# Root mean squares divided out after the projections instead of before the transposes

## The chip, the cores and the metric

The kernel runs on one core of one Trainium2 chip. The metric is the device time of one execution in microseconds (us). Five engines matter here: PE (TensorE, with its weight loads shown as PEld), DVE (VectorE), ACT (ScalarE), POOL (GpSimd) and SP, which issues most of the transfers.

## What is computed

Two stacks of blocks follow each other on 256 rows (tokens) of width 1024. Each block normalises its rows, multiplies them by one or more weight matrices, mixes them (state-space, recurrent, retention, sparse or cross attention, experts, or a gated feed-forward block) and adds the result to the rows. All arithmetic is float32. The norm ahead of a projection is

```
def rms_norm_2(x, g, eps=EPS):
    y = x * lax.rsqrt(jnp.mean(x * x, axis=-1, keepdims=True) + eps)
    return y * g

def swiglu(x, w_gate, w_up, w_down):
    return (jax.nn.silu(x @ w_gate) * (x @ w_up)) @ w_down
```

The factor `rsqrt(...)` is one number per row, and `g` one number per column of `x`. So the product `(x * r * g) @ w` equals `r * ((x * g) @ w)`: the factor per row may be applied before the product or to its result.

## The kernel before, in words

The rows lie in SBUF as `h`: 128 partitions, two token halves (`tt` = 0, 1), 1024 columns. A projection needs them transposed, with columns on the partitions; `normed` (L400) makes that. For each token half ACT squares and sums two halves of a row (L363), DVE adds them (L368), POOL raises the sum to the power -1/2 (L369), and DVE multiplies the identity by it, which gives the diagonal matrix `diag` (L409). PE then multiplies eight 128x128 blocks of `h` by `diag` (L411): each block comes out transposed and divided in one product. A float32 product takes two passes of PE, so the sixteen blocks of a norm are 32 records in the trace. Four PSUM banks of the small pool (`sm`, four banks) hold the eight transposed chunks. `put` (L382) then takes each chunk out of PSUM, multiplied by the column's gain, as two float32r parts: ACT writes the rounded value `xT_hi` (L385), DVE what is left, `xT_lo` (L386).

Weights stream from memory in units of 512 KB (L284). ACT rounds each unit to `whi` (L277, three buffers), and DVE takes the remainder `wlo` (L279, two buffers). `mm3` (L287) multiplies with three float32r products per chunk (L290, L291, L292). `fm_proj` (L294) gives results with columns on partitions, two units of 128 columns per PSUM bank; `tm_proj` (L309) gives them with rows on partitions, 512 columns per bank. Both hand a finished bank to an evacuation function. The large PSUM pool (`mm`) has four banks.

There are seventeen calls of `normed`. Eleven stand ahead of a projection touched here: `odd_mixer` (L793), two of `xattn` (L902), four of `ffn` (L1213), two of `xattn2` (L1263), `even_mixer2` (L1283) and `odd_mixer2` (L1626). The other six are the first mixer's, the two of the expert blocks and three for the memory rows. In the second stack each of the blocks but the last calls a `filler` after its norm: a piece of the keys' or values' projection of the memory, which does not depend on `h`.

The order of instructions on each engine is fixed when the program is built. A planner simulates the engines and, whenever an engine is free, gives it the ready instruction that comes first in the program (`later` shifts that position). On the chip each engine runs its own list strictly in that order and waits at semaphores, so an instruction that is ready later than the planner thought holds up all that stands behind it on its engine.

Of the kernel before, what the change touches and what calls it, by code (L numbers as in the profile page):

```python
# [9 lines left out]
F32 = mybir.dt.float32  # L10
# [11 lines left out]
P = 128  # L22
T = 256
# [181 lines left out]
class Kern:  # L205
# [159 lines left out]
    def row_rstd(self, ss, scale=1.0):  # L365

        r = self.small.tile([P, 1], F32, tag="rstd", name="rstd")
        self.nc.vector.tensor_scalar(r, ss[:, 0:1], ss[:, 1:2], EPS / scale ** 2, op0=ALU.add, op1=ALU.add)  # L368
        self.nc.gpsimd.tensor_tensor(r, r, self.mhalf[:, :1], op=ALU.pow)  # L369
        return r  # L370

    def rms_rows(self, src, tt):

        ss = self.small.tile([P, 2], F32, tag="ss", name="ss")
        for nb in range(2):
            self.square_sum(ss[:, nb:nb + 1], src[:, tt, nb * 512:nb * 512 + 512])
        return self.row_rstd(ss)
# [22 lines left out]
    def normed(self, src, gain, pool, name, dst=None):  # L400


        nc = self.nc
        dst = dst or self.parts(pool, 8, name)
        ps = [self.bank([P, 2, T]) for _ in range(4)]
        for tt in range(NT):
            r = self.rms_rows(src, tt)
            dg = self.small.tile([P, P], F32, tag="diag", name="diag")
            nc.vector.tensor_scalar(dg, self.ident, r, None, op0=ALU.mult)  # L409
            for c in range(8):  # L410
                nc.tensor.matmul(ps[c // 2][:, c % 2, tt * P:tt * P + P], src[:, tt, c * P:c * P + P], dg,  # L411
                                 start=True, stop=True)
        for c in range(8):
            self.put(dst, c, ps[c // 2][:, c % 2], self.col(gain, c))
        return dst

# [350 lines left out]
    def odd_mixer(self, norm_memory, filler):  # L767
        nc = self.nc
        with ExitStack() as es:
# [22 lines left out]
            with self.pool("odd_p") as pp:  # L792
                xT = self.normed(self.h, "norm_mix1", pp, "xT")  # L793

                def ev_f(j, ps, m):
                    nc.scalar.activation(kd[:, j:j + m], ps, AF.Sigmoid, scale=-1.0)
                    nc.scalar.activation(gc[:, j:j + m], ps, AF.Sigmoid)
                    for c in range(j, j + m):
                        nc.vector.tensor_scalar(kd[:, c], kd[:, c], om[:, c:c + 1], None, op0=ALU.mult)
                        nc.vector.tensor_scalar(gc[:, c], gc[:, c], om[:, c:c + 1], lb[:, c:c + 1],  # L800
                                                op0=ALU.mult, op1=ALU.add)
                self.fm_proj(xT, "od_f", range(8), ev_f)
                self.fm_proj(xT, "od_q", range(8),
                             lambda j, ps, m: nc.scalar.activation(qd[:, j:j + m], ps, AF.Silu))
# [21 lines left out]
                with self.later(200):  # L826
# [3 lines left out]
                self.tm_proj(xT, "od_i", lambda nb, tt, ps: nc.scalar.copy(  # L830
                    v[:, tt, nb * 512:nb * 512 + 512], ps))
                self.tm_proj(xT, "od_g", lambda nb, tt, ps: nc.scalar.activation(
                    gs[:, tt, nb * 512:nb * 512 + 512], ps, AF.Silu))
# [62 lines left out]
    def xattn(self, l, kT, v):  # L896
        nc = self.nc
        with self.pool("xa") as po:
            oT = self.parts(po, 8, "oT")
            with self.pool("xaq") as pq, self.pool("att_t", 2) as pt:  # L900
                qT = pq.tile([P, 8, T], F32, name="qT")
                xT = self.normed(self.h, f"norm_xattn{l}", pq, "xT")  # L902

                def head(j, ps, m):
                    nc.scalar.copy(qT[:, j:j + m], ps)
                    self.attend(j // 2, qT[:, j:j + 2], kT[:, j:j + 2], v, 1.0 / 16, oT, pt)
                self.fm_proj(xT, f"xa_q{l}", range(8), head)
            self.tm_proj(oT, f"xa_o{l}", self.add_to_h)
# [299 lines left out]
    def ffn(self, l, f, filler):  # L1208
        nc = self.nc
        with self.pool("ffn") as po:  # L1210
            aT = self.parts(po, 22, "aT")
            with self.pool("ffn_x") as px, self.pool("ffn_t", 2) as pt:
                xT = self.normed(self.h, f"ng{l}{6 if f else 0}", px, "xT")  # L1213
                filler()
                G, U = self.d(f"ff_g{l}{f}"), self.d(f"ff_u{l}{f}")
                for j in range(22):
# [6 lines left out]
                    a = pt.tile([P, T], F32, tag="a", name="a")  # L1223
                    nc.scalar.activation(a, ps[:, 0], AF.Silu)
                    nc.vector.tensor_tensor(a, ps[:, 1], a, op=ALU.mult)
# [31 lines left out]
    def xattn2(self, l, kT, v, filler):  # L1257
        nc = self.nc
        with self.pool("xa") as po:
            oT = self.parts(po, 4, "oT")  # L1260
            with self.pool("xaq") as pq, self.pool("att_t", 2) as pt:
                qT = pq.tile([P, 4, T], F32, name="qT")
                xT = self.normed(self.h, f"ng{l}4", pq, "xT")  # L1263
                filler()

                def heads(j, ps, m):
                    nc.scalar.copy(qT[:, j:j + m], ps)
# [5 lines left out]
    def even_mixer2(self, filler):  # L1273
        nc = self.nc
        with ExitStack() as es:
# [6 lines left out]
            with self.pool("ev2_x") as px, self.pool("ev2_raw", 2) as pr:  # L1282
                xT = self.normed(self.h, "ng02", px, "xT")  # L1283
                filler()
                with self.pool("rw_p") as pp:
                    rw = pp.tile([P, 14, T], F32, name="rw")

                    def shift(j, ps, m):
                        raw = pr.tile([P, 2, T + 1], F32, tag="raw", name="raw")
                        nc.vector.memset(raw[:, :, 0:1], 0.0)  # L1290
                        nc.scalar.copy(raw[:, :, 1:], ps)
# [6 lines left out]
                self.tm_proj(xT, "rt_qkv", lambda nb, tt, ps: nc.scalar.copy(  # L1298
                    qkv[:, tt, nb * 512:nb * 512 + 512], ps))
                self.fm_proj(xT, "rt_g", range(4), lambda j, ps, m: nc.scalar.activation(rg[:, j:j + m], ps, AF.Silu))  # L1300
# [319 lines left out]
    def odd_mixer2(self, filler):  # L1620
        nc = self.nc
        with self.pool("od2") as po:
            yT = self.parts(po, 8, "yT")
            pin = po.tile([P, NT, 456], F32, name="pin")
            with self.pool("od2_x") as px, self.pool("od2_t", 2) as pt:
                xT = self.normed(self.h, "ng12", px, "xT")  # L1626
# [5 lines left out]
                def ev_u(j, ps, m):  # L1632
                    t = pt.tile([P, T], F32, tag="t", name="t")
                    nc.scalar.copy(t, ps[:, 0])
                    nc.vector.tensor_tensor(u[:, j, 2:], ps[:, 1], t, op=ALU.mult)
# [7 lines left out]
                def ev_b(j, ps, m):  # L1643
                    for s in range(2):
# [4 lines left out]
                self.tm_proj(xT, "dsa_in", lambda nb, tt, ps: nc.scalar.copy(pin[:, tt], ps), n=456)  # L1649
# [162 lines left out]
```

## Time and profile before

| what | before |
|---|---|
| median of 3 runs (lowest to highest) | 3619.4 us (3611.51 to 3620.52) |
| the profiled execution | 3621.81 us |
| its span, first to last instruction | 3620.0 us |
| PE busy | 3510.9 us, 97% |
| DVE busy | 2404.2 us, 66% |
| ACT busy | 1781.6 us, 49% |
| mean granted clock of PE | 0.986 |

The shares are averages over very different stages. PE's records overlap, because its products are pipelined: one record of 256 columns lasts about 0.28 us, while the next starts some 0.12 us after it. A product of PE that waits for a semaphore shows as idle time of PE before it. The granted clock is 1.00 at the full 2.4 GHz and 0.50 at 1.2 GHz.

### The profile page before, as it was taken

What the parts mean: (1) busy time and instruction counts of PE and PEld (TensorE: products, weight loads), DVE (VectorE), ACT (ScalarE), POOL (GpSimd) and SP (SyncE); (2) the same over time, 40 slices, a digit from 0 to 9 for tenths busy, and PEclk for the clock granted to TensorE, in tenths of its full rate; (3) what the DMA queues carried; (4) which work ended last, traced back from release to release, by engine and by line L of the source; (5) the groups of instructions that cost most, each with busy time, mean ns of one, the idle gap of its engine ahead of it and who ended that gap; (6) DMA issues with size and microseconds to landing.
All of it is one profiled execution on the core that took longest, in us unless ns stands there. A gap on an engine that the chain in (4) does not pass through costs nothing. (4 is left out here: it accounts for less than half of the span.)

```text
span 3620.0 us, 60017 instructions
## 1 busy us (share of the span) xinstructions
PE 3510.9 (97%) x23584; PEld 3182.2 (88%) x23584; DVE 2404.2 (66%) x4051; ACT 1781.6 (49%) x2695; POOL 77.8 (2%) x93
## 2 busy tenths in 40 slices
PE   8999999999999999999999999999999999999899
PEld 8888999998888888899998888898898898987797
DVE  7655988977555754888986655555665555557554
ACT  6644444444444844445444444544523544444543
POOL 0000000000000000000000000000001000000000
PEclk9999999999999999999999999999998999999999
DMA  5444456668666544456668766566402455553355
GB/s 162 152 140 149 143 180 194 203 199 296 192 187 190 166 134 134 158 176 189 202 209 265 219 189 188 166 185 187 146 26 80 144 192 175 186 195 105 107 186 163
DMA packets 176835, 620.60 MB, mean 171 GB/s; under 512 B 19868, under 2 KB 20636, under 8 KB 175784
## 3 DMA queue, kind: packets, MB, share of 16 engines
q1 hardware_dynamic: 164000, 584.00, 52.0%
q10 hardware_dynamic: 12552, 32.78, 2.5%
q8 instruction: 184, 3.01, 0.3%
q14 instruction: 99, 0.81, 0.1%
HBM read 594.68 MB, written 22.02 MB: 170 GB/s over the span
## 5 line engine op out<-in xcount | busy, mean ns | idle before, releaser
L279 DVE TENSOR_TENSOR wlo<-wraw,whi 128x1024 fp32r<-128x1024 f32 x1058 | 1293.8, 1223 | 857.3 <-PE ps L292 316.3
L277 ACT CAST whi<-wraw 128x1024 fp32r<-128x1024 f32 x1058 | 1110.0, 1050 | 981.5 <-PE ps L291 705.4
L292 PE MATMUL ps<-xT_hi,wlo 128*128 128x256 f32 x4432 | 1253.5, 283 | 14.9 <-DVE wlo L279 14.0
L290 PE MATMUL ps<-xT_hi,whi 128*128 128x256 f32 x4432 | 1261.4, 285 | 0.9 <-ACT whi L277 0.8
L291 PE MATMUL ps<-xT_lo,whi 128*128 128x256 f32 x4432 | 1254.6, 283 | 0.5
L292 PEld LDWEIGHTS ps<-xT_hi,wlo 128*128 128x128 f32 x4432 | 836.1, 189 | 23.3 <-DVE wlo L279 21.3
L290 PEld LDWEIGHTS ps<-xT_hi,whi 128*128 128x128 f32 x4432 | 837.2, 189 | 5.5 <-ACT xT_hi L385 2.2
L291 PEld LDWEIGHTS ps<-xT_lo,whi 128*128 128x128 f32 x4432 | 836.9, 189 | 3.6 <-DVE xT_lo L386 2.3
L290 PE MATMUL ps<-whi,gh 128*128 128x512 f32 x1024 | 405.8, 396 | 3.6 <-ACT gh L1071 3.6
L291 PE MATMUL ps<-wlo,gh 128*128 128x512 f32 x1024 | 405.4, 396 | 0.0
L292 PE MATMUL ps<-whi,gl 128*128 128x512 f32 x1024 | 405.4, 396 | 0.0
L1071 ACT CAST gh<-H 128x256 fp32r<-128x256 f32 x256 | 104.1, 407 | 366.6 <-PE ps L291 364.7
L290 PEld LDWEIGHTS ps<-whi,gh 128*128 128x128 f32 x1024 | 193.3, 189 | 50.1 <-ACT gh L1071 4.0
L292 PEld LDWEIGHTS ps<-whi,gl 128*128 128x128 f32 x1024 | 193.3, 189 | 46.4 <-DVE gl L1073 0.5
L291 PEld LDWEIGHTS ps<-wlo,gh 128*128 128x128 f32 x1024 | 193.4, 189 | 46.0
L292 PE MATMUL ps<-whi,aT_lo 128*128 128x512 f32 x352 | 138.9, 395 | 0.0
L290 PE MATMUL ps<-whi,aT_hi 128*128 128x512 f32 x352 | 138.9, 394 | 0.0
L291 PE MATMUL ps<-wlo,aT_hi 128*128 128x512 f32 x352 | 138.8, 394 | 0.0
L1026 DVE TENSOR_TENSOR hot<-keys,i1T 128x1024 f16<-128x1024 f16 x64 | 130.4, 2037 | 0.0
L369 POOL TENSOR_TENSOR rstd<-rstd,mhalf 128x1 f32<-128x1 f32 x52 | 51.5, 990 | 2949.3 <-DVE rstd L368 2945.8
L1073 DVE TENSOR_TENSOR gl<-H,gh 128x256 fp32r<-128x256 f32 x256 | 107.4, 420 | 0.9 <-ACT gh L1071 0.9
L411 PE MATMUL ps<-diag,h 128*128 128x128 f32 x448 | 66.8, 317 | 42.3 <-DVE diag L409 39.8
(625 smaller groups left out, 4137.4 us busy)
## 6 DMA issues: line engine op xcount, KB each, us to landing
wraw<-in_peer_u_dram SPq DMA_DIRECT2D x256, 512.0 KB, 3.8
wraw<-in_peer_v_dram SPq DMA_DIRECT2D x256, 512.0 KB, 4.3
wraw<-in_ff_g_dram SPq DMA_DIRECT2D x88, 512.0 KB, 3.5
wraw<-in_ff_u_dram SPq DMA_DIRECT2D x88, 512.0 KB, 3.5
wraw<-in_ff_d_dram SPq DMA_DIRECT2D x88, 512.0 KB, 3.7
G<-late ACTq DMA_DIRECT2D x64, 320.0 KB, 4.5
g<-G SPq DMA_DIRECT2D x64, 320.0 KB, 4.9
wraw<-in_peer_q_dram SPq DMA_DIRECT2D x32, 512.0 KB, 3.6
```

What stands on the lines that cost most here:

```text
L277: nc.scalar.copy(hi, src)
L279: nc.vector.tensor_sub(lo, src, hi.bitcast(F32))
L290: mm(out, a[0], b[0], start=start, stop=False)
L291: mm(out, a[0], b[1], start=False, stop=False)
L292: mm(out, a[1], b[0], start=False, stop=stop)
L369: self.nc.gpsimd.tensor_tensor(r, r, self.mhalf[:, :1], op=ALU.pow)
L411: nc.tensor.matmul(ps[c // 2][:, c % 2, tt * P:tt * P + P], src[:, tt, c * P:c * P + P], dg, start=True, stop=True)
L1026: nc.vector.tensor_tensor(o1, keys[:, :, 0][:, None, :].to_broadcast([P, TOP, P]), i1T[:, t0:t0 + TOP, None].to_broadcast([P, TOP, P]), op ...
L1071: nc.scalar.copy(gh, src)
L1073: nc.vector.tensor_sub(gl, src, gh.bitcast(F32))
```

## The change

A new function `turned` takes the place of `normed` in eleven calls. It transposes the rows undivided, with PE's transposes against the identity, and puts them into the two parts with the gain as before. After that it makes `r`, the factor per row, with the same squares, sum and power. One product per token half with `r` spread over the stationary operand writes `r` along the free axis on all partitions, and ACT copies it to SBUF as `row`. It returns the transposed parts, `r` and a function `divide`.

Where a projection gives columns on partitions, `divide` multiplies the finished bank by `row` on DVE as it leaves PSUM. In `xattn`, `xattn2` and `even_mixer2` (`shift`) it takes the place of a copy on ACT; in `odd_mixer` (`ev_f`, `ev_q`), `even_mixer2` (`gate`), `ffn` and `odd_mixer2` (`ev_b`) it is an operation more; in `ev_u` it covers both halves of the bank, where before ACT copied one half. Where a projection gives rows on partitions, ACT's copy or Silu out of PSUM takes `r` as its scale per partition.

```
...
-    def row_rstd(self, ss, scale=1.0):
-        r = self.small.tile([P, 1], F32, tag="rstd", name="rstd")
+    def row_rstd(self, ss, scale=1.0, r=None):
+        r = self.small.tile([P, 1], F32, tag="rstd", name="rstd") if r is None else r
...
-    def rms_rows(self, src, tt):
+    def rms_rows(self, src, tt, r=None):
...
-        return self.row_rstd(ss)
+        return self.row_rstd(ss, 1.0, r)
...
+    def turned(self, src, gain, pool, name):
+        nc = self.nc
+        dst = self.parts(pool, 8, name)
+        for c in range(0, 8, 2):
+            ps = self.bank([P, 2, T])
+            for tt in range(NT):
+                for s in range(2):
+                    nc.tensor.transpose(ps[:, s, tt * P:tt * P + P], src[:, tt, (c + s) * P:(c + s) * P + P], self.ident)
+            for s in range(2):
+                self.put(dst, c + s, ps[:, s], self.col(gain, c + s))
+        r = pool.tile([P, NT], F32, name="r")
+        row = pool.tile([P, 1, T], F32, name="row")
+        ps = self.bank([P, T])
+        for tt in range(NT):
+            self.rms_rows(src, tt, r[:, tt:tt + 1])
+            nc.tensor.matmul(ps[:, tt * P:tt * P + P], r[:, tt:tt + 1].to_broadcast([P, P]), self.ident, start=True, stop=True)
+        nc.scalar.copy(row[:, 0], ps)
+        return dst, lambda tt: r[:, tt:tt + 1], lambda out, ps: nc.vector.tensor_tensor(
+            out, ps, row.to_broadcast([P, ps.shape[1], T]), op=ALU.mult)
...
-                xT = self.normed(self.h, "norm_mix1", pp, "xT")
+                xT, r, divide = self.turned(self.h, "norm_mix1", pp, "xT")
...
-                    nc.scalar.activation(kd[:, j:j + m], ps, AF.Sigmoid, scale=-1.0)
-                    nc.scalar.activation(gc[:, j:j + m], ps, AF.Sigmoid)
+                    f = gc[:, j:j + m]
+                    divide(f, ps)
+                    nc.scalar.activation(kd[:, j:j + m], f, AF.Sigmoid, scale=-1.0)
+                    nc.scalar.activation(f, f, AF.Sigmoid)
...
-                self.fm_proj(xT, "od_q", range(8),
-                             lambda j, ps, m: nc.scalar.activation(qd[:, j:j + m], ps, AF.Silu))
+                def ev_q(j, ps, m):
+                    divide(qd[:, j:j + m], ps)
+                    nc.scalar.activation(qd[:, j:j + m], qd[:, j:j + m], AF.Silu)
+                self.fm_proj(xT, "od_q", range(8), ev_q)
...
-                self.tm_proj(xT, "od_i", lambda nb, tt, ps: nc.scalar.copy(
-                    v[:, tt, nb * 512:nb * 512 + 512], ps))
+                self.tm_proj(xT, "od_i", lambda nb, tt, ps: nc.scalar.activation(
+                    v[:, tt, nb * 512:nb * 512 + 512], ps, AF.Copy, scale=r(tt)))
...
-                    gs[:, tt, nb * 512:nb * 512 + 512], ps, AF.Silu))
+                    gs[:, tt, nb * 512:nb * 512 + 512], ps, AF.Silu, scale=r(tt)))
...
-                xT = self.normed(self.h, f"norm_xattn{l}", pq, "xT")
+                xT, _, divide = self.turned(self.h, f"norm_xattn{l}", pq, "xT")
...
-                    nc.scalar.copy(qT[:, j:j + m], ps)
+                    divide(qT[:, j:j + m], ps)
...
-                xT = self.normed(self.h, f"ng{l}{6 if f else 0}", px, "xT")
+                xT, _, divide = self.turned(self.h, f"ng{l}{6 if f else 0}", px, "xT")
...
-                    a = pt.tile([P, T], F32, tag="a", name="a")
-                    nc.scalar.activation(a, ps[:, 0], AF.Silu)
-                    nc.vector.tensor_tensor(a, ps[:, 1], a, op=ALU.mult)
+                    gu = pt.tile([P, 2, T], F32, tag="gu", name="gu")
+                    divide(gu, ps)
+                    a = gu[:, 0]
+                    nc.scalar.activation(a, a, AF.Silu)
+                    nc.vector.tensor_tensor(a, gu[:, 1], a, op=ALU.mult)
...
-                xT = self.normed(self.h, f"ng{l}4", pq, "xT")
+                xT, _, divide = self.turned(self.h, f"ng{l}4", pq, "xT")
...
-                    nc.scalar.copy(qT[:, j:j + m], ps)
+                    divide(qT[:, j:j + m], ps)
...
-                xT = self.normed(self.h, "ng02", px, "xT")
+                xT, r, divide = self.turned(self.h, "ng02", px, "xT")
...
-                        nc.scalar.copy(raw[:, :, 1:], ps)
+                        divide(raw[:, :, 1:], ps)
...
-                self.tm_proj(xT, "rt_qkv", lambda nb, tt, ps: nc.scalar.copy(
-                    qkv[:, tt, nb * 512:nb * 512 + 512], ps))
-                self.fm_proj(xT, "rt_g", range(4), lambda j, ps, m: nc.scalar.activation(rg[:, j:j + m], ps, AF.Silu))
+                self.tm_proj(xT, "rt_qkv", lambda nb, tt, ps: nc.scalar.activation(
+                    qkv[:, tt, nb * 512:nb * 512 + 512], ps, AF.Copy, scale=r(tt)))
+                def gate(j, ps, m):
+                    divide(rg[:, j:j + m], ps)
+                    nc.scalar.activation(rg[:, j:j + m], rg[:, j:j + m], AF.Silu)
+                self.fm_proj(xT, "rt_g", range(4), gate)
...
-                xT = self.normed(self.h, "ng12", px, "xT")
+                xT, r, divide = self.turned(self.h, "ng12", px, "xT")
...
-                    t = pt.tile([P, T], F32, tag="t", name="t")
-                    nc.scalar.copy(t, ps[:, 0])
-                    nc.vector.tensor_tensor(u[:, j, 2:], ps[:, 1], t, op=ALU.mult)
+                    t = pt.tile([P, 2, T], F32, tag="t", name="t")
+                    divide(t, ps)
+                    nc.vector.tensor_tensor(u[:, j, 2:], t[:, 0], t[:, 1], op=ALU.mult)
...
+                    divide(cy[:, j - 4:j - 2], cy[:, j - 4:j - 2])
...
-                self.tm_proj(xT, "dsa_in", lambda nb, tt, ps: nc.scalar.copy(pin[:, tt], ps), n=456)
+                self.tm_proj(xT, "dsa_in", lambda nb, tt, ps: nc.scalar.activation(
+                    pin[:, tt], ps, AF.Copy, scale=r(tt)), n=456)
...
```

## Rows read from the trace of the kernel before

**Rows 1.** The profile's page, engines: busy us, share of the span, instructions

```profile
PE 3510.9 (97%) x23584; PEld 3182.2 (88%) x23584; DVE 2404.2 (66%) x4051; ACT 1781.6 (49%) x2695; POOL 77.8 (2%) x93
```

**Rows 2.** Waits of PE, whole span: who, for whom, us in total, times, longest

```profile
PE ps L411 <- DVE diag L409: 39.8, 13, 9.4
PE ps L292 <- DVE wlo L279: 16.9, 29, 2.9
...
PE ps L411 <- DVE rstd L368: 2.5, 3, 1.1
```

**Rows 3.** Timeline of PE at norms: start, us, engine, line, shapes, count [idle before, releaser]

```profile
288.08 3.76 PE L411 MATMUL ps<-diag,h 128*128 128x128 f32 x31 [1.93 <-DVE diag L409]
...
357.95 3.71 PE L411 MATMUL ps<-diag,h 128*128 128x128 f32 x30 [1.93 <-DVE diag L409]
...
1193.11 2.89 PE L411 MATMUL ps<-diag,h 128*128 128x128 f32 x16 [3.57 <-DVE diag L409]
1196.34 2.49 PE L411 MATMUL ps<-diag,h 128*128 128x128 f32 x15 [0.34 <-DVE diag L409]
...
2304.83 6.41 PE L411 MATMUL ps<-diag,h 128*128 128x128 f32 x32 [7.75 <-DVE diag L409]
...
2843.16 4.04 PE L411 MATMUL ps<-diag,h 128*128 128x128 f32 x32 [0.97 <-DVE diag L409]
...
3417.22 6.59 PE L411 MATMUL ps<-diag,h 128*128 128x128 f32 x32 [8.49 <-DVE diag L409]
```

**Rows 4.** Timeline of PE, one set of sixteen transposes

```profile
145.11 1.91 PE L396 MATMUL ps<-ident,ybuf 128*128 128x128 f32 x16
```

**Rows 5.** Timeline of DVE, last writes of the rows ahead of four norms

```profile
287.14 0.68 DVE L345 TENSOR_TENSOR h<-ps,h 128x512 f32<-128x512 f32 x1
...
1189.15 1.28 DVE L345 TENSOR_TENSOR h<-ps,h 128x512 f32<-128x512 f32 x2
...
2302.23 1.41 DVE L1184 SCALAR_TENSOR_TENSOR h<-h,rstd,g 128x512 f32<-128x512 f32 x2 [0.73 <-POOL rstd L369]
...
3414.61 1.42 DVE L1204 SCALAR_TENSOR_TENSOR h<-y,rstd,h 128x512 f32<-128x512 f32 x2 [0.44 <-POOL rstd L369]
```

**Rows 6.** Timeline of POOL, two of four powers at one norm

```profile
2509.41 1.40 POOL L369 TENSOR_TENSOR rstd<-rstd,mhalf 128x1 f32<-128x1 f32 x1 [1.72 <-DVE rstd L368]
2512.53 0.55 POOL L369 TENSOR_TENSOR rstd<-rstd,mhalf 128x1 f32<-128x1 f32 x1 [1.72 <-DMA masks<-in_c_masks_dram]
```

**Rows 7.** Groups by line, 2500 to 2560: busy us, mean ns, idle before

```profile
L1291 ACT COPY raw<-ps 128x512 f32<-128x512 f32 x6 | 3.5, 578 | 0.0
...
L386 DVE SCALAR_TENSOR_TENSOR xT_lo<-ps,cols,xT_hi 128x256 fp32r<-128x256 f32 x8 | 3.4, 479 | 1.3 <-ACT xT_hi L385 1.3
...
L1199 DVE TENSOR_TENSOR y<-ps,g 128x512 f32<-128x512 f32 x2 | 1.4, 689 | 2.5 <-ACT junk L363 2.5
```

**Rows 8.** Timeline of DVE in a feed-forward block, one pair of weight units

```profile
2350.25 1.22 DVE L279 TENSOR_TENSOR wlo<-wraw,whi 128x1024 fp32r<-128x1024 f32 x1 [1.71 <-PE ps L292]
2351.47 0.42 DVE L1225 TENSOR_TENSOR a<-ps,a 128x256 f32<-128x256 f32 x1
2352.37 0.43 DVE L1227 TENSOR_TENSOR aT_lo<-a,aT_hi 128x256 fp32r<-128x256 f32 x1 [0.47 <-ACT aT_hi L1226]
2353.07 1.23 DVE L279 TENSOR_TENSOR wlo<-wraw,whi 128x1024 fp32r<-128x1024 f32 x1 [0.28 <-PE ps L292]
```

**Rows 9.** Stretches: busy (instructions) PE, PEld, DVE, ACT, POOL; PEclk, DMA, GB/s

```profile
145.00:147.00 2.00, 2.00 (x19) 1.90 (x18) 0.48 (x1) 1.14 (x3) 0.00 (x0) 1.00 0.36 51
1194.20:1197.50 3.30, 2.96 (x14) 2.67 (x14) 0.71 (x3) 2.27 (x7) 1.10 (x2) 0.50 0.25 101
2300.10:2310.20 10.10, 5.37 (x25) 5.37 (x26) 4.44 (x13) 6.25 (x17) 2.75 (x5) 0.50 0.36 123
2320.00:2420.00 100.00, 100.00 (x836) 100.00 (x835) 56.73 (x70) 49.43 (x70) 0.00 (x0) 1.00 0.61 182
3412.80:3423.00 10.20, 5.79 (x27) 5.79 (x28) 4.08 (x10) 2.59 (x8) 2.50 (x3) 0.50 0.17 51
```

## The prediction

> **What bounds the kernel now.** I read the page's engine line first: PE is busy for 3510.9 of 3620.0 us [rows 1], so the end is set by how much PE has to do and by 109 us in which it stands. The list of PE's waits comes next. Its longest entries are the diagonal matrix of the norms and the remainder of the weights, `wlo` [rows 2]. The norms' entries are 39.8 and 2.5 us, 42.3 in all. Of these 9.4 us is the first norm of the program and 3.9 us belongs to the two expert blocks (1.93 in the row at 357.95, which stands for two), and neither is changed [rows 2, 3]. That leaves 29.0 us of waiting ahead of the eleven changed norms.
>
> The third view is PE's timeline at those norms [rows 3]. Each shows an idle piece, then 32 passes in one block. At the full clock the block lasts 4.04 us, a pass every (4.04 - 0.28) / 31 = 0.121 us, so 3.9 us. Where the granted clock is at 0.50 it lasts up to 6.6 us [rows 3, 9]. The reader is to see that the idle pieces are of two kinds: about 1 us or less where a filler stands beside the norm (the row at 2843.16 stands for six such norms), and 2 to 8.5 us where none is at hand (288, 1193, 2305, 3417, and xattn of layer 1, which looks like 288).
>
> **The change part by part.**
>
> *Transposes for products.* Sixteen transposes take the place of sixteen two-pass products. One such set in this trace lasts 1.91 us for 16 records, a transpose every (1.91 - 0.27) / 15 = 0.109 us, so 1.75 us [rows 4]. The product that spreads `r` is new: two products, four passes, 0.48 us. Per norm PE's work falls by 3.9 - 1.75 - 0.48 = 1.67 us, over eleven norms by 18.4 us. This lies on the path, since PE is the bound.
>
> *The wait.* The first product of a projection no longer needs squares, sum, power and diagonal; it needs the last write of `h`, the late transposes and one `put`. What it cost is late next in another place: the product that spreads `r` waits for the same squares and power, and behind it in PE's list stand the projection's products. The trace has no such product. Its wait is bounded by nothing (the first bank is only evacuated two units, 5.6 us, after the products begin, so there is room) and by 1.93 us, the wait of a norm whose chain is fully exposed [rows 3]. The powers last 0.55 or 1.40 us [rows 6]; an order fixed in advance meets one of them wrongly, and I take the difference, 0.85 us, once per norm.
>
> With a filler (six norms) I leave the present idle time, 0.3 to 1.1 us, where it is: the same lateness only moves to the new product. The gain is the 1.67 us of work, less 0.3 us because the first `put` now has a shorter row of passes to hide behind: 1.4 us each, 8.4 us.
>
> Without a filler the chain itself becomes shorter.
> - At 288 the first product of the projection comes when the block of L411 ends, about 291.8. `h` is final at 287.82 [rows 5]; DVE then makes the first lower part in 0.48 us [rows 7], so products can start at 288.3. That is 3.5 us, less 0.48 and 0.85 for the new product: 2.2 us. Twice, with layer 1: 4.4 us.
> - At 1193 the block ends at 1198.8 and `h` is final at 1190.43 [rows 3, 5]. A split of 1.22 us and other work stand on DVE and ACT, so I put the first product at 1193.0: 5.8 us, less 1.33: 4.5 us.
> - At 2305 the block ends at 2311.2, `h` is final at 2303.64; late transposes at the low clock and a `put` take 2 us, so 5.6 us. But PE's clock stands at 0.50 until 2310.2 [rows 9], after an idle piece of 7.75 us that stays in large part, so the earlier products run at half speed for 4.6 us and lose 2.3. Less 1.33: 2.0 us.
> - At 3417 it is the same: block to 3423.8, `h` at 3416.03, products from 3417.9, 5.9 us, less 2.55 us for 1.2 GHz until 3423.0 [rows 9], less 1.33: 2.0 us.
>
> *The evacuations.* `divide` is a DVE operation on 128x512 from PSUM; the nearest row takes 0.69 us [rows 7], two of 128x256 would take 0.84 [rows 8]. I take 0.69, as it has the same shape. It is issued 123 times: 88 in the four `ffn`, 8 in `odd_mixer`, 9 in `even_mixer2`, 8 in `xattn`, 4 in `xattn2`, 6 in `odd_mixer2`: 85 us on DVE (103 at the other end), against 23 ACT copies of 0.58 us saved. Its cover is PE's stream: in 100 us of feed-forward PE is busy for all 100, DVE for 57 [rows 9]. The order there shows how much room there is [rows 8]: the split begun at 2350.25 serves the unit that starts one unit, 2.82 us, later, and is first needed by that unit's third product, at 2353.07 + 0.24. `divide` behind the split, then Silu, product and lower part still end before that unit is split. So I cost it at nothing there. In the attention projections' last pair there is no cover; four of them pay 0.1 us each, or up to 1.3 where a split stands ahead. I take 1.3 us for all together.
>
> *Nothing else moves the end.* The diagonal matrices leave DVE; eleven copies of `row` come to ACT, which is busy for half of the span. ACT's copies with a scale are the same operation. No transfer is added, removed or delayed by more than the projections themselves.
>
> *A rule against it.* The sixteen transposes at 145 ran at a granted clock of 1.00 after PE had been busy without a gap [rows 9]. The Trainium skill (TensorE: Matmul & The Clock Gate, Part 4: PE-mode transpose) says that the full clock does not engage for transposes. This trace does not show that; by the rule the rival on the clock below would come true, 3611 us in place of 3599.
>
> **The sum.** 8.4 + 4.4 + 4.5 + 2.0 + 2.0 - 1.3 = 20.0 us. The profiled execution took 3621.8 us, 1.8 more than its span, and is 2.4 us above the median; the difference is carried over to the median: 3619.4 - 20.0 = 3599.4, so 3599 us. Its own range, with the new product's wait between 0 and 1.93 us (+9.4 to -11.9 us), is 3590 to 3611.
>
> **The rivals.**
> - *The waits go altogether.* The planner fills the chain with products of the projection itself, which are ready now. Then 18.4 us of work and most of the 29.0 us of waits go: 3572 at the extreme, 3578 with a few us left. For it: the projection's first two units have 5.6 us before anything needs `row`. Against it: at six norms a filler was ready as well, and PE waited about 1 us all the same.
> - *The new product takes the place of the old wait.* The planner puts it right behind the transposes, and PE stands there for the whole chain, 1.93 us in place of 0.85 at all eleven norms: 12 us less gain, 3611 us. For it: it comes before the projection in the program. Against it: the planner only issues what it holds ready.
> - *Transposes leave the clock low.* Seven of the eleven norms run at 1.00 now. If PE's waiting and transposing brings each a stretch at 0.50 like that from 1194.2 to 1197.5, after an idle piece of 3.57 us [rows 3, 9], half of 3.3 us is lost seven times: 11.6 us, 3611 us. Against it: the set at 145.
> - *DVE becomes late in the feed-forward blocks.* If the planner puts `divide`, product and lower part all ahead of the split at 2350.25, the split starts 0.69 + 0.47 + 0.42 + 0.47 + 0.43 = 2.48 us later, ends at 2353.95 and is needed at 2353.31: PE stands 0.64 us in each of 88 pairs, 56 us. The kernel is then slower, 3655 us; it decides from 31 pairs on (20 / 0.64). For it: they come before the next weights in the program. Against it: the planner takes what is ready, and before this change it put the split first [rows 8].
>
> **How the numbers follow.** The forecast has a chance of 0.54, the waits going altogether 0.14, the new product's wait 0.12, the clock 0.08, DVE late 0.12 (with half to all of the pairs, 3627 to 3655). No change is what lies within 0.3%, 10.9 us, about what a measurement of this kernel can tell: 3608.5 to 3630.3. Faster: 0.54 + 0.14 = 0.68; same: 0.12 + 0.08 = 0.20; slower: 0.12. The range from 3574 to 3622 leaves out the extreme of the first rival and most of the last.
>
> **What would show it.** In the profile after: at the eleven norms a block of 16 transposes of about 1.9 us; the waits for the diagonal down from 42.3 us to about 13, and a new entry of 5 to 15 us for the product that spreads `r`; the first product of the projection at 3417 about 1.5 to 2 us after the last write of `h`; DVE some 75 us busier and `wlo` waits still near 17 us. The prediction is wrong if PE's busy time has not fallen by some 15 us, if `wlo` waits grow by 20 us or more, or if stretches at half clock appear at norms that had none.

## The result, and the profile after

The changed kernel takes 3585.23 us (median of 6 runs, 3579.68 to 3595.49), the kernel before 3619.94 us beside it (6 runs, 3611.51 to 3620.53): ratio 0.9912, 95% interval 0.9894 to 0.993. The gain is 34.7 us where the sum gave 20.0. The sign held, and so did both sources of the gain, less work for PE and shorter waits; the size was too small, and the sections below say which term.

The page's engine line after the change:

```profile
PE 3496.6 (97%) x23452; PEld 3170.2 (88%) x23452; DVE 2452.7 (68%) x4152; ACT 1777.1 (49%) x2684; POOL 74.8 (2%) x93
```

Against [rows 1] PE is busy for 14.3 us less; the span, 3593.6 us, is 26.4 us shorter, so PE also stands idle for 12.1 us less (109.1 before, 97.0 after). DVE is busy for 48.5 us more. Next, PE's waits, whole span (line numbers have moved: L426 is the new transpose, L434 the product that spreads `r`, L1211 and L1231 write `h`):

```profile
PE ps L292 <- DVE wlo L279: 14.9, 26, 2.5
PE ps L411 <- DVE diag L409: 13.5, 4, 9.3
PE ps L426 <- DVE h L1231: 7.8, 13, 3.0
PE ps L434 <- POOL r L369: 5.4, 8, 1.1
...
PE ps L426 <- DVE h L1211: 4.0, 2, 3.7
```

The diagonal's entries went from 42.3 us [rows 2] to the 13.5 us of the norms that were not changed. In their place stand 11.8 us in which the transposes wait for `h` itself and 5.4 us for the spreading product. Norm by norm, PE's idle time ahead of these products fell from 24.0 to 10.8 us at the five norms without a filler; at the six with one it rose from 5.0 to 7.2 us, 4.2 of them at the spreading product. The waits for `wlo` have not grown.

The timeline of PE at two norms without a filler answers to the rows at 288 and 1193 of [rows 3]:

```profile
286.66 1.47 PE L426 MATMUL ps<-ident,h 128*128 128x128 f32 x12
288.55 0.39 PE L290 MATMUL ps<-xT_hi,whi 128*128 128x256 f32 x1 [0.42 <-ACT xT_hi L385]
288.77 0.60 PE L426 MATMUL ps<-ident,h 128*128 128x128 f32 x4
...
290.49 0.68 PE L434 MATMUL ps<-ident,r 128*128 128x128 f32 x4 [0.23 <-DVE xT_lo L386]
```
```profile
1188.45 2.04 PE L426 MATMUL ps<-ident,h 128*128 128x128 f32 x16
1190.24 0.36 PE L290 MATMUL ps<-xT_hi,whi 128*128 128x256 f32 x1
1191.24 0.39 PE L291 MATMUL ps<-xT_lo,whi 128*128 128x256 f32 x1 [0.63 <-DVE xT_lo L386]
```

The idle 1.93 and 3.57 us ahead of these norms are gone, the sixteen transposes last about 2 us, and the spreading product stands behind the first products, 0.23 us late at the first of the two and 0.98 us, in two pieces, at the second. The last norm, with the last write of `h` ahead of it, answers to the rows at 3417 and 3414 of [rows 3, 5]; PE first, then DVE:

```profile
3390.70 1.97 PE L426 MATMUL ps<-ident,h 128*128 128x128 f32 x8 [3.02 <-DVE h L1231]
3394.41 1.97 PE L426 MATMUL ps<-ident,h 128*128 128x128 f32 x8 [1.74 <-DVE h L1231]
3396.02 0.77 PE L290 MATMUL ps<-xT_hi,whi 128*128 128x256 f32 x2
...
3399.65 0.49 PE L434 MATMUL ps<-ident,r 128*128 128x128 f32 x2 [0.24 <-POOL r L369]
```
```profile
3393.60 1.41 DVE L1231 SCALAR_TENSOR_TENSOR h<-y,rstd,h 128x512 f32<-128x512 f32 x2 [0.44 <-POOL rstd L369]
```

Half of the transposes run while the second half of the rows is still being written. The first product comes 1.0 us after the last write of `h` (3396.02 against 3395.01); before it came 7.5 us after (3423.56, as the passes end, against 3416.03).

Stretches of the kernel after (busy us of PE, PEld, DVE, ACT, POOL; granted clock; DMA share; GB/s) answer to [rows 9]:

```profile
1188.00:1190.20 2.20, 2.20 (x18) 1.91 (x17) 2.20 (x5) 0.98 (x3) 0.00 (x0) 1.00 0.87 331
2288.20:2295.00 6.80, 6.32 (x28) 5.86 (x29) 5.23 (x12) 4.12 (x11) 0.55 (x1) 0.50 0.44 157
3390.70:3397.50 6.80, 5.06 (x22) 4.52 (x23) 5.81 (x11) 4.50 (x13) 1.94 (x2) 0.50 0.34 113
2691.00:2728.50 37.50, 37.50 (x204) 34.35 (x203) 12.42 (x25) 4.00 (x10) 3.65 (x6) 0.50 0.00 1
```

The transposes at 1188 ran at the full 2.4 GHz. At 2288 and 3391 the clock is at its lower level, 1.2 GHz, as it was before, but for 6.8 us in place of 10.2. A second profile of the changed kernel has 6.8 us again at the first of them and 10.2 at the last:

```profile
3386.30:3396.60 10.30, 7.98 (x36) 7.45 (x37) 8.27 (x17) 6.17 (x18) 2.49 (x3) 0.50 0.26 96
```

The row at 2691 is a stage whose own work the change doesn't touch: 37.5 us at half clock in this execution and 13.6 more right behind, where the trace of before has 34 us in three pieces. Such stretches come and go between runs of one kernel, and they have to be taken out before two kernels a few us apart can be compared.

Two ways do that, and both are used below. *From the runs:* each of 138 executions lists its mean granted clock. Within one kernel, 0.001 less clock goes with 2.7 us more time (one slope for all; the single kernels' own mostly lie between 2.2 and 4.1); the six runs of the changed kernel lie between 3579.68 us at 0.991 or 3580.79 at 0.992 and 3595.49 at 0.986. "At equal clock" means a kernel's mean time brought to 0.987 with that slope; single runs then scatter by about 2 us, and the kernel before, with 53 runs, is at 3619.4 us, the changed one, with 11, at 3591.0. So 28.4 us of the gain are the kernel's at equal clock; the other 6 go with the clock of the changed kernel's first six runs, 0.9892 in the mean (2.2 x 2.7 = 5.9). Equal clock takes out half clock whatever brought it, also what an edit itself brings or saves. At the eleven norms the trace of before has 27.3 us at half clock (3.4 us at 1194 and at 1392, 10.2 at 2300 and at 3413), the two profiles of the change have 13.7 and 20.5. So the 28.4 us leave out a part of what the change gains; without any correction the means of all runs, 3618.6 and 3586.9 us, differ by 31.8. *From the profile:* in each stretch of 1 us, PE's busy time times (1 - granted clock) is what a busy PE lost to the half clock. Busy time less that loss is PE's work at full clock, and the rest of the span is standing:

| profiled execution | span | work at full clock | lost to half clock | standing |
|---|---|---|---|---|
| before | 3620.0 | 3470.1 | 40.8 | 109.1 |
| after | 3593.6 | 3451.4 | 45.2 | 97.0 |
| after, second profile | 3590.5 | 3453.9 | 40.9 | 95.7 |
| e1, transposes as two-pass products | 3587.9 | 3471.0 | 26.8 | 90.1 |
| e2, transposes wait for `r` | 3616.1 | 3449.4 | 50.5 | 116.2 |
| e3, divides by ones on the old norms | 3631.0 | 3469.4 | 47.6 | 114.0 |
| e4, only the six norms with filler | 3607.5 | 3457.4 | 42.5 | 107.6 |
| e5, only the five without | 3605.4 | 3464.9 | 41.6 | 98.9 |
| e6, no chain of factors | 3581.4 | 3449.0 | 39.5 | 92.9 |
| e7, four more norms turned | 3590.8 | 3451.0 | 36.5 | 103.3 |
| e8, spreading product later | 3586.0 | 3451.9 | 37.8 | 96.3 |
| e9, e3 without the stage of `ng12` | 3630.7 | 3466.8 | 51.8 | 112.1 |
| e10, after with `ng12` as before | 3587.0 | 3454.9 | 34.8 | 97.3 |

Each row is one execution, and kernels with the same passes differ by up to 3 us in the second column, which is about its accuracy. Before to after: 18.7 us of work and 12.1 us of standing.

### The profile page after: what moved, and what is told of

Same layout as the page of the kernel before. It is cut to its first block, busy times and chain, and to the rows that moved or that the text cites. A ratio compares the mean times of both kernels' runs of the same rounds, so it can differ in the third digit from the quotient of the medians.

```text
span 3593.6 us, 59809 instructions
## 1 busy us (share of the span) xinstructions
PE 3496.6 (97%) x23452; PEld 3170.2 (88%) x23452; DVE 2452.7 (68%) x4152; ACT 1777.1 (49%) x2684; POOL 74.8 (2%) x93
## 5 line engine op out<-in xcount | busy, mean ns | idle before, releaser
L292 PEld LDWEIGHTS ps<-xT_hi,wlo 128*128 128x128 f32 x4432 | 836.1, 189 | 24.4 <-DVE wlo L279 22.1
L436 DVE TENSOR_TENSOR gu<-ps,row 128x512 f32<-128x512 f32 x88 | 60.9, 692 | 128.3 <-PE ps L292 128.2
L1056 DVE TENSOR_TENSOR hot<-hot,gT 128x1024 f16<-128x1024 f16 x128 | 82.9, 692 | 0.0
```

Source lines behind the costliest of these rows:

```text
L292: mm(out, a[1], b[0], start=False, stop=stop)
L436: return dst, lambda tt: r[:, tt:tt + 1], lambda out, ps: nc.vector.tensor_tensor(out, ps, row.to_broadcast([P, ps.shape[1], T]), op=ALU.mult)
L1056: nc.vector.tensor_tensor(og[:, k], o2, bc(gT[:, k]), op=ALU.mult)
```

## The experiments

Runs of the kernel before stood beside each group: 3618.82 us (19 runs) with e1, e2, e3 and the repeat, 3619.86 (17) with e4, e5, e6 and e8, 3616.7 (17) with e7, e9 and e10.

**The changed kernel again.**

> The changed kernel once more, beside the experiments on the same chip. Expected 3579 to 3596 us, 0.991 of before, as in its first six runs. It is the yardstick for the other three: each theory's figure below is to be read against it.

3588.88 us (3581.99 to 3592.82), ratio 0.9911 [0.9895, 0.9928]. The gain repeats, and this is the run to which the three others of its group are compared.

**From before to after in three steps: e3, then e2, then the change.** e3 keeps the old norms and adds the divisions alone, by ones:

```
-        for c in range(0, 8, 2): ... nc.tensor.transpose(...) ... self.put(...)
+        dst = self.normed(src, gain, pool, name)
...
+        nc.vector.memset(r, 1.0)
+        nc.vector.memset(row, 1.0)
```

> The kernel before with the new evacuations alone: norms as before, divide multiplies by a row of ones and ACT scales by ones, both from memsets. Theory that PE's stream covers them: 3620 to 3623 us, no difference that can be measured. Rival, DVE becomes late in the feed-forward blocks: 0.64 us per pair where the order is bad, 3627 to 3676. Rival, the new order of evacuation is itself worth something: 3612 or less.

3632.1 us (3626.18 to 3636.3), ratio 1.0034 [1.0021, 1.0047], so 13 us slower. At equal clock it is 3622.4, so 3.0 us slower; its runs had a mean clock of 0.9836 against 0.9871 for before. At equal clock the divisions cost little, and most of the 13 us go with half clock. All seven runs had a low one (0.982 to 0.986), so it belongs to this kernel's time; that the divisions bring it is not shown, and the changed kernel, with the same divisions, has 0.9885 in the mean. Of the 4.9 us more that PE stands in e3's profile (table), 4.7 are waits for `wlo` (26.8 us in all against 22.1), and the growth lies outside the feed-forward blocks.

e2 makes the transposes wait again, by an identity matrix that is made from `r` (a comparison of `ident * r` with zero), and with it the old order, in which both token halves are transposed ahead of the first `put`; the rest of the change stays:

```
+            dg = self.small.tile([P, P], F32, tag="diag", name="diag")
+            nc.vector.tensor_scalar(dg, self.ident, r[:, tt:tt + 1], 0.0, op0=ALU.mult, op1=ALU.is_gt)
+            for c in range(8):
+                nc.tensor.transpose(ps[c // 2][:, c % 2, ...], src[:, tt, c * P:c * P + P], dg)
```

> The changed kernel with transposes that wait as the products did before: squares, power, and an identity that is made from the row's factor (the comparison of factor times identity with zero), one per token half, then eight transposes of that half; the evacuations and the new product stay. Theory (18.4 us of work, the rest of the gain from the chain): 3585 + 16 = 3601 us, and the waits for the diagonal come back near 29 us at the eleven norms. Rival, the work is all and the chain is worth nothing: 3585 to 3588. Rival, the chain is nearly all: 3610 or more.

3620.17 us (3609.1 to 3625.79, 12 runs), ratio 1.0002 [0.9991, 1.0013]: with the wait back the whole gain is gone in the medians. At equal clock 3611.2 us: 20.2 of the 28.4 us are gone. Equal clock leaves out what half clock at the norms costs, and e2's profile has 37.5 us of it there, the change's two 13.7 and 20.5. The groups of PE's instructions (busy, mean ns, idle before and its releaser) show where, e2 first, then the change:

```profile
L429 PE MATMUL ps<-diag,h 128*128 128x128 f32 x176 | 30.5, 335 | 35.6 <-DVE diag L427 35.3 <-DVE r L368 0.3
```
```profile
L426 PE MATMUL ps<-ident,h 128*128 128x128 f32 x176 | 29.5, 307 | 11.7 <-DVE h L1231 7.8 <-DVE h L1211 4.0
L434 PE MATMUL ps<-ident,r 128*128 128x128 f32 x44 | 9.7, 309 | 6.3 <-POOL r L369 5.4 <-DVE xT_lo L386 0.7
```

The same 176 transposes stand 35.6 us behind the diagonal, or 11.7 us behind `h` with 6.3 us at the new product. In the kernel before these norms waited 29.0 us, so e2 waits some 6 us more than before. The two pull opposite ways, and what the wait alone is worth in the change is known only to some us. The rival that the wait is nearly all of the gain comes nearest. It is not all: e2 still does 20 us less work than e3 (table), but stands 2.2 us more, and at equal clock it is 11.2 us faster.

**e1, the passes alone.** The sixteen transposes are two-pass products with the undivided identity, without any wait for `r`:

```
-                    nc.tensor.transpose(ps[:, s, ...], src[...], self.ident)
+                    nc.tensor.matmul(ps[:, s, ...], src[...], self.ident, start=True, stop=True)
```

> The changed kernel with its sixteen transposes per norm made as two-pass float32 products against the identity, nothing else. Theory that PE's work is the largest part: each norm gets 3.9 - 1.75 = 2.15 us of passes back, eleven times 23.6 us, so about 3609 us. Rival, that the chain is what was gained and the passes lie in waiting time: at the five norms without a filler half of the passes run while PE waits for the second token half anyway, so 6 x 2.15 + 5 x 1.1 = 18 us at most, and if the filler norms hide them too, under 8 us: 3593 us or less. Rival on the clock (transposes leave it low): the products would hold the clock up and the time would not rise at all.

3598.02 us (3589.65 to 3599.29), ratio 0.9944 [0.993, 0.9958]; 3602.0 at equal clock, 11.0 above the change. The 176 passes are there (17 to 20 us more work than in the two profiles of the change), but PE stands 6 to 7 us less. Its waits for `h` are 10.5 us where the change has 11.8, those at the spreading product 3.8 where it has 6.3: a share of the passes lies where PE would have waited anyway, so work and waits can't be summed as if each were on the path. The time lies between the two figures expected, 3609 and 3593 or less.

**e4 and e5, the norms by kind.** Old functions are put back for the five norms without a filler (e4), or for the six with one (e5).

```
 e4:  odd_mixer, xattn, ffn(0,0), ffn(1,1) from the kernel before
 e5:  xattn2, even_mixer2, odd_mixer2, ffn(0,1), ffn(1,0) from the kernel before
```

> The change at the six norms with a filler beside them alone (even_mixer2, odd_mixer2, both xattn2, two ffn); the other five norms and their evacuations as before. The prediction's terms say 8.4 us, so 3611 us. If the gain at these norms is more than the saved passes (waits shrink too), 12 us or more: 3608 or less. If the waits only move, as predicted, between 6 and 10 us.

> The change at the five norms without a filler alone (odd_mixer, both xattn, the first and the last ffn); the other six as before. The prediction's terms say 12.9 us, so 3607 us. By the trace after, which shows about 22 us at these five, 3598 us. Together with the run of the other six the two gains should add up to that of the whole change, some 34 us; if they don't, the rest is an effect of the order of work as a whole or of the clock.

e4: 3615.6 us (3608.44 to 3626.54, 12 runs), ratio 0.9991 [0.9976, 1.0005]. e5: 3600.36 us (3594.64 to 3607.17), ratio 0.9939 [0.9926, 0.9952]. By medians they gain 4 and 20 us, 6 to 11 less than the whole (29.9 and 34.7 us in its two groups of runs). At equal clock it is 3608.9 and 3604.1, gains of 10.5 and 15.3, 25.8 in sum against 28.4; in the table 14.2 and 15.4, against 29.6 to 30.8. e4's runs had a mean clock of 0.9842. So the two parts nearly add up, and what seemed lost between them is half clock. A third reading sets each product of the projections against the same one of before: how much further it is ahead behind a norm than in front of it is that norm's gain, whatever the clock does elsewhere. It gives 11.2 us at the six norms of e4 and 21.0 at the five of e5, 32.2 in sum, and 31.0 and 32.5 in the two profiles of the change. e5's 15.3 at equal clock are fewer because this counts the half clock that the change saves at its norms. The standing shows their difference in kind: e4 takes 1.5 us of it away, e5 10.2.

**e6, the chain of factors.** Squares, power, spreading product and its copy are left out at the eleven norms, with ones in their place; the result of this kernel lacks the division.

```
-            self.rms_rows(src, tt, r[:, tt:tt + 1])
-            nc.tensor.matmul(ps[...], r[:, tt:tt + 1].to_broadcast([P, P]), self.ident, start=True, stop=True)
-        nc.scalar.copy(row[:, 0], ps)
+        nc.vector.memset(r, 1.0)
+        nc.vector.memset(row, 1.0)
```

> The changed kernel with the chain of the row's factor left out in the eleven norms: no squares, no power, no spreading product; factor and row are ones from memsets, so the division is left out of the result. Theory: what is left of the chain costs the four passes, 0.48 us x 11 = 5.3 us, and the waits for the factor, 5.4 us in the trace after: 10.7 us less than the changed kernel, about 3574 us. Rival, PE has other work to do meanwhile and only the passes count: 3580. Rival, the squares on ACT also delay the puts: 3570 or less.

3584.72 us (3583.3 to 3584.86), ratio 0.9903 [0.9888, 0.9917]; 3583.7 at equal clock, 7.3 below the change. So the whole chain, the spreading product's work and wait included, costs some 7 us, between two of the gains expected, 5 and 10.7. There were four runs, and by medians they are only 0.5 and 4.2 us below the change's two groups.

**e8, the spreading product forty places later in the order.**

```
+        with self.later(40):
             for tt in range(NT): nc.tensor.matmul(...)
             nc.scalar.copy(row[:, 0], ps)
```

> The changed kernel with the product that spreads the factor, and ACT's copy of it, put 40 places later in the planner's order, so that products of the projection go ahead of it. Theory: the waits of PE for the factor, 5.4 us in the trace after, go, and nothing else changes: 3580 us. Rival: the wait only moves to the first evacuation or to DVE and the time stays at 3585, or the order around it becomes worse: 3588 or more.

3587.9 us (3579.81 to 3592.79), ratio 0.991 [0.9895, 0.9924], and 3589.2 at equal clock, 1.8 below the change: no clear difference. But the edit hardly made the order that was to be tried. Of the 6.3 us of idle time ahead of this product 5.6 are still there, most of them in this entry (the product is L436 here):

```profile
PE ps L436 <- POOL r L369: 5.2, 7, 1.1
```

Only at both `xattn` norms and the last one does the product stand further back, where it had waited 0.7 us in all, and there the wait is gone. At the other eight it stands behind as many instructions of PE as in the change. Whether a later place would recover the rest of the wait is not shown.

**e9 and e10, where the divisions cost.** The profile has DVE nearly as busy as PE in the sparse-attention part of the stage behind `ng12` (13.05 and 13.52 of 13.60 us in the first row below; DVE is not the busiest engine there, as the expectations have it), and e3's products fell back most there. e9 is e3, e10 the changed kernel, each with this stage taken from the kernel before:

```
-                    divide(t, ps)
-                    nc.vector.tensor_tensor(u[:, j, 2:], t[:, 0], t[:, 1], op=ALU.mult)
+                    nc.scalar.copy(t, ps[:, 0])
+                    nc.vector.tensor_tensor(u[:, j, 2:], ps[:, 1], t, op=ALU.mult)
```

> The kernel that keeps the old norms and divides the projections' results by ones (it measured 3632.1 us, 13 above the kernel before), with the short-convolution and sparse-attention stage (norm ng12) taken whole from the kernel before. Theory A: the cost of the divides sits in that one stage, where the profile has VectorE the busiest engine: the time falls to 3619-3623 us. Theory B: the cost is spread over all ten other places (the 88 divides in the feed-forward blocks above all): it stays at 3628-3632.

> The changed kernel with the norm ng12 and its stage as before (diagonal products, result copied by ScalarE). By theory A (the divides cost some 10 us in that stage, the turned norm gains 1.4 to 5 there): 3576-3583 us, 5 to 10 below the changed kernel (3588). By theory B: the turned norm's gain is lost and no divide's cost comes back: 3589-3593. If the stage is as fast either way because the earlier rows pay for the divides: 3585-3590.

e9: 3624.65 us (3616.56 to 3632.45, 12 runs), ratio 1.0019 [1.0008, 1.0031]. e10: 3586.01 us (3581.88 to 3593.31), ratio 0.9918 [0.9903, 0.9933], no gain over the change. At equal clock e9 is at 3620.9, 1.5 us slower than before, and e10 at 3593.2, 2.2 us above the change. So at equal clock the other divisions, the 88 of the feed-forward blocks among them, cost some 1.5 us, and those of this stage some 1.5, which its turned norm more than pays for. Neither theory held as put, since both had taken the 13 us for the divisions' own; e10's median lies in the third case, as fast either way. One profile shows where most of e9's loss was. The same stage, unchanged in e9, before and then e9, which is some 4.5 us behind as the slow stretch begins (columns as above):

```profile
3277.00:3290.60 13.60, 13.52 (x98) 11.55 (x96) 13.05 (x47) 7.80 (x17) 1.84 (x2) 1.00 0.26 79
```
```profile
3265.00:3277.00 12.00, 12.00 (x64) 9.80 (x63) 2.42 (x6) 6.00 (x15) 0.00 (x0) 0.99 0.14 45
3277.00:3290.60 13.60, 13.60 (x38) 8.60 (x38) 8.05 (x30) 4.45 (x11) 0.29 (x1) 0.50 0.06 10
```

PE was busy for all of the 12 us before, as it was in the kernel before, then in e9 the clock fell to half, for 17.1 us in all (3276.8 to 3293.9), and PE did 38 instructions in 13.6 us. The kernel before passes the same code at 1.00. Set product against product, e9 falls back by some 7 us here. What makes such a stretch likelier in e3, e4 and e9 (mean clock 0.9836 to 0.9854) than in before (0.9873) stays open.

**e7, four more norms turned** (the first mixer's and the three of the memory), their projections' results scaled as they leave PSUM:

```
-                xT = self.normed(self.h, "norm_mix0", pp, "xT")
+                xT, r, divide = self.turned(self.h, "norm_mix0", pp, "xT")
```

> The changed kernel with four more norms turned (the first mixer's and the three of the memory). If what is gained is the chain of squares, sum and power ahead of the first product, and each such norm had that chain bare: 3578-3583 us. If their chains lie beside other TensorE work, as at the norms with a filler: 3586-3590.

3596.24 us (3592.6 to 3603.82), ratio 0.9952 [0.9937, 0.9967], slower than the change; 3597.7 at equal clock, 6.7 us worse. The first product came 5 us earlier (10.5 us into the span in place of 15.6), but by 130 us its products stood 11 us behind those of the change. PE's waits of e7 in the first 130 us:

```profile
PE ps L426 <- DMA h<-in_x_dram: 6.1, 2, 4.8
PE ps L291 <- DVE wlo L279: 3.1, 1, 3.1
PE ps L292 <- DVE wlo L279: 2.4, 2, 1.8
```

The two waits for `wlo` were 0.3 us in all in the change, and three stretches of 3.4 us at half clock came with them. So some 5 of the 11 us are waits for the weights' remainder, and up to 5 the 10.2 us at half clock; that the divisions on DVE made the remainder late is argued, not shown. At the first norm of the memory its products gain nothing on those of the change, at the other two about 0.9 and 1.4 us. Neither this nor any other kernel tried beats the change by more than the runs scatter, e6 aside, which leaves out the division.

## Why the prediction was too small

**The work: right in amount, too dear in the sum.** The sum took 18.4 us off PE's passes. The page shows 14.3; with the half clock taken out it is 18.7, and 16.2 by the second profile. But "this lies on the path" holds for about half of it: giving passes back costs 11.0 us, not 23.6 (e1), because some of them fit into waits, and with the wait still there the shorter passes were worth 11.2 us (e3 to e2).

**The waits: mis-sized, and this is the failed term.** The gains of the norms come to 21.3 us, of which 18.4 are work, so the prediction left 2.9 us for all waits and the half clock at the norms together. PE's standing fell by 12.1 us, and e2, which puts the wait back, stands 19.2 us more and is 20.2 us slower at equal clock. Set product against product, the norms gain 31.0 and 32.5 us in the two profiles of the change and 4.1 in e2's. So the sum had two errors of opposite sign, work too dear and waits far too cheap, and that it still came to 20.0 is in part luck. Three numbers in the waits failed:
- *The new product's wait.* 0.85 us was the difference of two powers' durations [rows 6]. The text takes it "once per norm", and the range varies it at all eleven; the sum itself charges it at the five bare norms, 4.3 us. There the product waits 2.1 us (0.23, 0.98, 0.23, 0.41 and 0.24), because the planner put products of the projection ahead of it. At the norms with a filler it waits 4.2 us. Work and wait of the whole chain cost some 7 us at equal clock (e6), where eleven times 0.48 + 0.85 would be 14.6.
- *The last and the first feed-forward norm, 2.0 us each.* The sum let the half clock last as long as before. It lasted 6.8 us in place of 10.2 at both in the first profile and at the first of them in the second, and at the last the first product came 1.0 us behind `h`, not 1.9. Product against product their gains are 4.6 to 5.4 us (last, the smaller with 10.2 us at half clock) and 4.0 (first) in the two profiles of the change.
- *The second `xattn` norm, 2.2 us.* It was taken for like the first, but [rows 3] shows only the first; in the trace of before a half-clock stretch of 3.4 us begins at 1392 (rows below), and it is gone in both profiles of the change. Product against product the gain is 4.2 us. At the first `xattn` norm 3.2 us stand against 2.2, at 1193 3.7 to 4.5 against 4.5.

```profile
1391.23 5.46 PE L411 MATMUL ps<-diag,h 128*128 128x128 f32 x32 [1.94 <-DVE diag L409]
```
```profile
1392.10:1395.50 3.40, 3.40 (x18) 3.40 (x17) 0.29 (x1) 0.28 (x1) 0.55 (x1) 0.50 0.43 143
```

By kind, the five bare norms gain 15.3 us (e5 at equal clock), or 19.7 to 21.2 product against product, where 12.9 were summed, and the six with a filler 10.5 or 11.3 where 8.4 were. That waits stay where they are at a norm with filler is nearly borne out: e4 takes only 1.5 us of standing away, and the idle time at transposes and spreading product is 7.2 us where the diagonal's was 5.0.

**The divisions: a little too cheap.** 1.3 us was taken; e3 costs 3.0 at equal clock, and 13 with the half clock that came with it. In a feed-forward block DVE's order, with ACT's part, answers to [rows 8]:

```profile
2345.03 0.69 DVE L436 TENSOR_TENSOR gu<-ps,row 128x512 f32<-128x512 f32 x1 [1.50 <-PE ps L292]
2345.63 1.22 DVE L279 TENSOR_TENSOR wlo<-wraw,whi 128x1024 fp32r<-128x1024 f32 x1
2345.91 0.41 ACT L1253 ACTIVATE gu<-gu 128x256 f32<-128x256 f32 x1
2346.77 0.42 DVE L1254 TENSOR_TENSOR gu<-gu 128x256 f32<-128x256 f32 x1
...
2347.66 0.43 DVE L1256 TENSOR_TENSOR aT_lo<-gu,aT_hi 128x256 fp32r<-128x256 f32 x1 [0.47 <-ACT aT_hi L1255]
...
2348.00 1.22 DVE L279 TENSOR_TENSOR wlo<-wraw,whi 128x1024 fp32r<-128x1024 f32 x1
```

The division did go ahead of the split, not behind it as the prediction had it, but alone: the product and the lower part wait for Silu and let the split pass. The split starts 0.60 us behind the division's start, and PE's waits for `wlo` have not grown (14.9 against 16.9 us). The rival of a late DVE needed 2.48 us ahead of the split and did not come. The divisions' durations come to 85 us, as forecast; DVE's busy time rose by 48.5 and not by 75, since neighbouring records overlap and busy time counts an overlap once; all of DVE's durations together rose by 87.5.

**The other rivals.** *The waits go altogether* came nearest of them: its reason, products of the projection fill the chain, is what the rows at 288 and 3399 show, but 18 us are left at transposes and spreading product. *The new product in place of the old wait* is refuted by its 5.4 us. *Transposes leave the clock low* is refuted by the rows: of the seven norms that ran at 1.00 before none shows a half-clock stretch as it transposes, in either profile of the change, and the sets at 286.66 and 1188.45 ran at 1.00. (e2's transposes have such a stretch at 290, but so have the old products at that norm in e4, at 289.) The Trainium skill (TensorE: Matmul & The Clock Gate, Part 4: PE-mode transpose) says that transposes don't get the full clock engaged; by that rule the rival would have held, and the row of 1188.00, with 18 records in 2.20 us at 1.00, does not agree. Whether transposes alone would raise a low clock no run here shows.

**What would show it, point by point.** Blocks of about 1.9 us: 2.04 at 1188, two pieces of 1.97 at 3391, and at the norms with a filler sixteen transposes among other products, over about 5 us. Diagonal waits to about 13: 13.5. A new entry of 5 to 15 us: 5.4. First product 1.5 to 2 us behind `h` at the last norm: 1.0. DVE 75 us busier: 48.5. `wlo` waits near 17: 14.9. PE's busy time down by 15: 14.3.

## What to carry to other kernels

A factor per row commutes with the projection, so it can be divided out behind it; what that buys is above all that the statistics' chain leaves the path of the first product, most where nothing else is at hand to fill it (standing fell by 10.2 us at the five norms that were bare of other work, by 1.5 at the six with a filler). Price the wait of a newly added consumer by what can run ahead of it, not once per place by the length of its producer. And before two kernels some 10 us apart are compared, set each run's granted clock beside its time: here 13 us of "cost of the divisions" were 3 at equal clock. What the clock takes out still has to be accounted for: part of it can be the edit's own, as with the half clock that this change saves at its norms.

## What the runs showed that was not expected

- Runs of one kernel scatter with the granted clock, by 2.7 us per 0.001; with that taken out the scatter falls to about 2 us (138 runs, 12 kernels).
- A stretch at half clock came in the midst of steady work: 17.1 us long in e9, after 12.0 of 12.0 us busy, in code that the kernel before passes at 1.00. The longest in these traces is the 37.5 us at 2691.
- Two edits that seemed not to add up by 6 to 11 us (e4 and e5) do so within 3 us at equal clock, and product against product within the spread of the two profiles of the change.
